# Layer A's output weights split ahead of time and kept in DRAM, and the bias rows of heads 4 to 15 written at another place

## The chip, the cores and the metric

The kernel runs on one core of one Trainium2 chip. The time is device microseconds (us) of one execution. Engines are called as in the profile: PE multiplies matrices (PEld is its weight load, which lies beside the matmuls), DVE, ACT and POOL work on vectors, SP here only issues DMAs. PE, DVE, ACT and POOL each work through their own instructions in order; so do the queues on which SP and POOL issue DMAs.

## The reference

A decoder of two layers over 1024 tokens of 1024 numbers, in float32. Layer A attends in three ways at once (over compressed blocks of keys, over chosen blocks, over a sliding window), adds the gated sum of the three through an output matrix, and runs a SwiGLU. Then one K/V is projected for layer B, whose heads attend over windows of three dilations. What the change touches is in these lines:

```python
def nsa_attention(h, w_in, ..., w_out, rel_bias):
    proj = h @ w_in                      # q, keys and values, gates
    ...
    k_cmp = compress(kvh(kc), pe_k, w1_k, w2_k)   # gelu(blocks @ w1) @ w2
    v_cmp = compress(kvh(vc), pe_v, w1_v, w2_v)
    ...                                  # every logit gets rel_bias[t5_bucket(distance)]
    o = g[..., 0:1] * o_cmp + g[..., 1:2] * o_sel + g[..., 2:3] * o_win
    return o.reshape(B, S, D_MODEL).astype(h.dtype) @ w_out
```

## The kernel before, in words

**Splits.** Every operand of a matmul is held as a high part (a rounded copy, made by ACT: `split` L139, `Pairs` L762) and a low part (operand minus high part, made by DVE: L140, L763; in a few places POOL). `mm3` (L166 to L168) makes one product of three matmuls: high by high, high by low, low by high.

**Order of the work.** The kernel is written as Python that records instructions. A scheduler then moves them within their dependencies by a model of the time. So the place of a call in the code isn't its place on an engine; where it stands there is shown below by rows of the order itself.

**Projections (0 to about 285 us).** `x` is normalised and turned, then multiplied by the column blocks of `a_w_in`. Weights come through the class `Weights`: SP loads 512 KB into a ring of three `wraw` tiles (L155), ACT and DVE split it into rings of five `wh` and `wl`. `tok_proj` makes values token by token (eight tiles of 128 tokens; 304 columns with the gates, then 256 columns); each tile is evacuated from one of six `mm` banks of PSUM by an ACT copy into `vt` (a ring of two), which POOL's queue stores to DRAM (`vS`). `compress` (L395 on) loads the compression weights in four quarters of 512 KB (`in_a_w_k_dram` in the rows below), makes for each of 16 chunks a split operand `bh`, `bl` (L410, L411) and adds six matmuls of 256 columns per chunk into the banks `cmp0` and `cmp1`; after them come the gelu (`hid`) and a second product.

**The bias rows.** `bias_rows` makes the bias by distance for all heads with four small matmuls (L252) and POOL's queue stores it to DRAM as `sR` (L254). `bias_skewed` (L256) then copies, for two heads at a time, one row of `sR` 128 times into the tensor `sA`, from which the attention reads slanted tiles (`T<-sA`). Each of the eight calls is one DMA of 1151 KB from DRAM to DRAM on SP's queue (L263). The argument `prev` ties it to a weight load: it can't be issued before that one.

**Attention A (about 285 to 745 us).** `jobs()` walks 32 units of four groups and eight tiles of tokens; a unit is `(g, t)`.

**Output product of A (about 745 to 845 us).** `out_proj` (L1048) loads `a_w_out` as eight tiles `ow`, and `rows_steps` (L789) multiplies the attention's output `oT` (left blocks) by `ow` (right blocks) in a recursion of seven products instead of eight. Each operand block of 128x512 goes through `Pairs` before use. Products three and four take sums of blocks: POOL makes them, four instructions on `oT` and four on `ow` (into `tb` or in place) for each product's preparation, L829 to L839. Results are added into `xr` by DVE (L821). The same function serves layer B later. The SwiGLU of layer A follows, and its first steps are placed among the recursion's last.

Of the kernel before, what the change touches and what calls it, by code (L numbers as in the profile page):

```python
# [10 lines left out]
F32 = mybir.dt.float32  # L11
F32R = mybir.dt.float32r
# [9 lines left out]
NT = S // 128  # L22
# [8 lines left out]
LA, L1, L2 = 1151, 511, 255  # L31
# [60 lines left out]
def trunk(ctx, tc, I, out):  # L92
    nc = tc.nc
# [249 lines left out]
    with ExitStack() as c:  # L343
# [95 lines left out]
        def evac_v(i):  # L439
# [6 lines left out]
            return f  # L446

        bias_rows(cp)
# [54 lines left out]
        for _ in steps:  # L503
            pass
        cctx.close()

# [11 lines left out]
    with ExitStack() as c:  # L518
# [190 lines left out]
        def jobs():  # L709
# [78 lines left out]

    def rows_steps(spare, pairs, tmp, blocks, xr):  # L789

# [3 lines left out]

        def step(ops, onX, where, sums=None, whole=False, eng=(None, None)):
# [29 lines left out]
        def sums1(i, a, b):  # L825
            (a11, a21, a12, a22), (b11, b12, b21, b22) = a, b
            tA.append(tmp("a", i))
            tB.append(tmp("b", i))
            nc.gpsimd.tensor_add(tA[i], a21, a22)  # L829
            nc.gpsimd.tensor_sub(tB[i], b12, b11)  # L830
            nc.gpsimd.tensor_sub(a21, a11, a21)
            nc.gpsimd.tensor_sub(b12, b22, b12)

        def sums2(i, a, b):
            (a11, a21, a12, a22), (b11, b12, b21, b22) = a, b
            nc.gpsimd.tensor_sub(tA[i], tA[i], a11)
            nc.gpsimd.tensor_sub(tB[i], b22, tB[i])
            nc.gpsimd.tensor_sub(a12, a12, tA[i])
            nc.gpsimd.tensor_sub(b21, b21, tB[i])  # L839

# [3 lines left out]
        T = lambda i: tA[i], lambda i: tB[i]  # L844
        return [step((A(0), B(0)), 1, [(0, 0)]),
                step((A(2), B(2)), 0, [(0, 0)]),
                step(T, 0, [(1, 1), (0, 1)], sums1),
                step(T, 2, [(0, 1)], sums2),
                step((A(2), B(3)), 0, [(0, 1)]),
                step((A(1), B(1)), 2, [(1, 1)], eng=(None, P)),  # L850
                step((A(3), B(2)), 2, [(1, 0)], whole=True, eng=(P, None))]

# [196 lines left out]
    def out_proj(pw, pp, p, xr, oT, w, x_src, norm):  # L1049
        raw = {k: pw.tile([128, 1024], F32, name=f"ow{k}") for k in (3, 7, 0, 4, 1, 5, 2, 6)}  # L1050
        for i in range(4):
            nc.sync.dma_start(raw[i], w[i * 128:(i + 1) * 128, :])
        for i in range(4):
            nc.sync.dma_start(xr[:, i, :], x_src[i * 128:(i + 1) * 128])
            nc.sync.dma_start(raw[i + 4], w[(i + 4) * 128:(i + 5) * 128, :])
        for t in range(4, NT):
            nc.sync.dma_start(xr[:, t, :], x_src[t * 128:(t + 1) * 128])
        lo, hi = slice(0, 512), slice(512, 1024)
        blocks = [((oT[:, i, lo], oT[:, i, hi], oT[:, i + 4, lo], oT[:, i + 4, hi]),
                   (raw[i][:, lo], raw[i][:, hi], raw[i + 4][:, lo], raw[i + 4][:, hi])) for i in range(4)]  # L1060
        steps = rows_steps(("dr0", "dr1", "ux", "uy"), Pairs(pp, 6),
                           lambda s, i: p.tile([128, 512], F32, name=f"t{s}{i}"), blocks, xr)
        staged(steps[:6] + [norm] + steps[6:])
# [301 lines left out]

    dense(0, I["a_w_out"][0], x_in, oT, (begin_B, project_B), "left", "right")
    oT_ctx.close()
# [297 lines left out]
```

## Time and profile before

| | us |
|---|---|
| time of three runs | 3013.38, 3022.8, 3020.68 (median 3020.68) |
| the profiled execution's own time | 3014.07 |
| its span in the profile | 3012.3 |
| PE busy | 2869.0 (95%) |
| DVE busy | 2405.6 (80%) |
| ACT busy | 1600.7 (53%) |
| POOL busy | 1640.1 (54%) |

The views used are: windows (busy time of each engine, with the count of instructions, in a stretch of time; behind them the mean granted clock of PE as a share of full speed, the busy share of the 16 DMA engines, and GB/s), groups (all instructions of one line, engine and shape: busy time, mean ns of one, and the idle time ahead of them with what ended it), tiles (count, then shortest/mean/longest ns, then first and last start), the timeline (start, length, engine, instruction; in brackets the idle time before it and what ended it), and DMA issues (count, KB of each, median us from issue to landing).

### The profile page before, as it was taken

Reading aid. Unit: us, or ns where it says so; the run is one execution under the profiler, and the core shown is the slowest. Engines: PE = TensorE matmul, PEld = TensorE weight load, DVE = VectorE, ACT = ScalarE, POOL = GpSimd, SP = SyncE. Lnnn points to the kernel's source line nnn. Section 1 sums busy time; section 2 is a strip of 40 time slices with the busy share of each in tenths; the row PEclk is TensorE's granted clock in tenths of the full one; section 3 lists DMA queues with packets and bytes.
Section 4 is the critical chain, followed back from the end, with each engine's and each line's share of the span. In section 5 each row is a group of like instructions: output and inputs, shape, how many; then the busy total and the mean of one; then the engine's idle time right before and its main releaser. Section 6 shows DMA issues by size and latency. Waiting matters only on the chain.

```text
span 3012.3 us, 44147 instructions
## 1 busy us (share of the span) xinstructions
PE 2869.0 (95%) x14670; PEld 2378.2 (79%) x14670; DVE 2405.6 (80%) x4832; ACT 1600.7 (53%) x3596; POOL 1640.1 (54%) x1751
## 2 busy tenths in 40 slices
PE   7999999999889999999999999899988999999997
PEld 6988888888667878888777788788866778888886
DVE  4432888988988898898875677588899788889887
ACT  5432888887363333333364444689964533333334
POOL 2134666666766555555556787333347655555551
PEclk9999999999999999999999999999999999999999
DMA  6765032121212223222124555866520212111111
GB/s 171 221 193 167 24 105 79 33 60 58 73 51 65 64 63 78 67 58 72 56 94 143 157 164 149 267 199 183 147 95 25 63 49 63 53 53 57 56 46 74
DMA packets 266196, 293.43 MB, mean 97 GB/s; under 512 B 17971, under 2 KB 209347, under 8 KB 265968
## 3 DMA queue, kind: packets, MB, share of 16 engines
q1 hardware_dynamic: 246320, 230.45, 26.6%
q0 software_dynamic: 19648, 60.16, 6.6%
q8 instruction: 116, 1.90, 0.3%
q14 instruction: 112, 0.92, 0.1%
HBM read 227.44 MB, written 78.81 MB: 102 GB/s over the span
## 4 chain that ended last, share of the span: by engine, by line
PE 61%; DVE 22%; ACT 6%; issue 5%; DMA 3%; POOL 2%; SPq 1%; DVEq 0%; ACTq 0%; POOLq 0%
DVE pl L763 7%; PE ux L166 5%; DVE xr L821 5%; PE ux L167 5%; PE ux L168 4%; PE pt L276 4%; PE uy L166 4%; PE uy L167 4%; PE uy L168 4%; PE dx L167 3%; PE mm L166 3%; PE dx L168 3%; PE mm L167 3%; PE mm L168 2%; PE dr L166 2%
## 5 line engine op out<-in xcount | busy, mean ns | idle before, releaser
L763 DVE TENSOR_TENSOR pl<-oT,ph 128x512 fp32r<-128x512 f32 x315 | 333.7, 1079 | 40.8 <-ACT ph L762 34.6
L762 ACT ACTIVATE ph<-oT 128x512 fp32r<-128x512 f32 x329 | 198.8, 626 | 222.3 <-PE ux L167 58.5
L276 PE MATMUL pt<-ident,P 128*128 128x128 f32 x1536 | 244.5, 278 | 10.9 <-ACT P L1459 2.7
L763 DVE TENSOR_TENSOR pl<-oTb,ph 128x512 fp32r<-128x512 f32 x229 | 228.1, 1021 | 24.0 <-ACT ph L762 23.9
L762 ACT ACTIVATE ph<-oTb 128x512 fp32r<-128x512 f32 x239 | 143.1, 625 | 185.4 <-PE ux L167 51.4
L821 DVE TENSOR_TENSOR xr<-xr,dr 128x512 f32<-128x512 f32 x336 | 214.4, 678 | 28.2 <-PE dr L168 28.1
L140 DVE TENSOR_TENSOR tl<-pt,th 128x512 fp32r<-128x512 f32 (+1 forms) x320 | 206.9, 651 | 30.8 <-ACT th L139 28.7
L821 DVE TENSOR_TENSOR xr<-xr,dx 128x512 f32<-128x512 f32 x352 | 220.1, 676 | 2.9 <-PE dx L168 2.2
L167 PE MATMUL dx<-pl,ph 128*128 128x512 f32 x512 | 203.2, 401 | 9.7 <-DVE pl L763 8.6
L689 POOL TENSOR_SCALAR P<-P,sm,gates 128x384 f32<-128x384 f32 (+7 forms) x256 | 182.5, 724 | 54.1 <-DVE sm L687 48.2
L276 PEld LDWEIGHTS pt<-ident,P 128*128 128x128 f32 x1536 | 179.6, 142 | 29.9 <-ACT P L1459 6.7
L168 PE MATMUL dx<-ph,pl 128*128 128x512 f32 x512 | 199.9, 397 | 0.3 <-DVE pl L763 0.3
L139 ACT ACTIVATE th<-pt 128x512 fp32r<-128x512 f32 (+1 forms) x320 | 176.8, 563 | 41.1 <-PE pt L276 35.2
L685 ACT ACTIVATE P<-P,m 128x384 f32<-128x384 f32 (+7 forms) x256 | 170.8, 669 | 16.2 <-DVE m L683 8.2
L1082 POOL TENSOR_TENSOR oT<-oT,gffn 128x512 f32<-128x512 f32 x92 | 108.2, 1183 | 128.7 <-DMA oT<-in_ffn_w_up_dram 112.4
L166 PE MATMUL dx<-ph 128*128 128x512 f32 x512 | 157.3, 398 | 8.4 <-DVE xr L821 3.3
L1082 POOL TENSOR_TENSOR oTb<-oTb,gffn 128x512 f32<-128x512 f32 x92 | 106.1, 1160 | 92.6 <-DMA oTb<-in_ffn_w_up_dram 83.1
L299 PE MATMUL o<-tl,V 128*128 128x256 f32 x540 | 147.6, 298 | 8.4 <-POOL tl L292 4.4
L298 PE MATMUL o<-th,V 128*128 128x256 f32 x540 | 149.6, 294 | 2.4 <-ACT th L139 1.3
L291 POOL TENSOR_SCALAR th<-traw 128x128 fp32r<-128x128 f32 (+1 forms) x112 | 74.8, 671 | 126.9 <-ACT traw L290 46.3
L1459 ACT ACTIVATE P<-P,st 128x384 f32<-128x384 f32 (+2 forms) x256 | 139.5, 547 | 7.7 <-PE pt L1570 4.1
L167 PEld LDWEIGHTS dx<-pl,ph 128*128 128x128 f32 x512 | 97.5, 190 | 40.7 <-DVE pl L763 21.1
(617 smaller groups left out, 9547.6 us busy)
## 6 DMA issues: line engine op xcount, KB each, us to landing
qB<-xr POOLq DMA_DIRECT2D x96, 256.0 KB, 4.9
oT<-in_ffn_w_up_dram SPq DMA_DIRECT2D x92, 256.0 KB, 3.0
oTb<-in_ffn_w_up_dram SPq DMA_DIRECT2D x92, 256.0 KB, 3.0
Q<-qB SPq DMA_DIRECT2D x40, 512.0 KB, 8.2
wd<-in_ffn_w_down_dram SPq DMA_DIRECT2D x66, 256.0 KB, 2.7
oT<-in_b_w_q_dram SPq DMA_DIRECT2D x48, 256.0 KB, 3.4
K<-kBs SPq DMA_DIRECT2D x40, 256.0 KB, 10.3
wraw<-in_a_w_in_dram SPq DMA_DIRECT2D x18, 512.0 KB, 5.0
```

Source lines behind the costliest of these rows:

```text
L139: nc.scalar.activation(H_, src, AF.Copy)
L140: nc.vector.tensor_sub(L_, src, f32(H_))
L166: nc.tensor.matmul(ps, lh, rh, start=first, stop=False, skip_group_check=bool(shared))
L167: nc.tensor.matmul(ps, lh, rl, start=False, stop=False, skip_group_check=bool(shared))
L168: return nc.tensor.matmul(ps, ll, rh, start=False, stop=last, skip_group_check=bool(shared))
L276: nc.tensor.transpose(ps[:, i * 128:(i + 1) * 128], b, ident)
L685: nc.scalar.activation(P[:, e, :n], P[:, e, :n], AF.Exp, bias=mm[:, e:e + 1], scale=-1.0, accum_out=sm[:, e:e + 1])
L689: nc.gpsimd.tensor_scalar(P[:, e, :n], P[:, e, :n], sm[:, e:e + 1], gt(g, t, br, 2 * hp + e, 1), op0=OP.mult, op1=OP.mult)
L762: nc.scalar.activation(h, src, AF.Copy)
L763: (eng or nc.vector).tensor_sub(l, src, f32(h))
L821: nc.vector.tensor_add(xs, xs, banks[t])
L1082: nc.gpsimd.tensor_mul(v, v, gains[:, k:k + 4].unsqueeze(2).to_broadcast([128, 4, 128]))
```

## The change

There are two parts.

First, a generator `prepared_out` runs in the projections. In four rounds it loads two tiles of `a_w_out` (`po0`, `po1`, 512 KB each, on SP), makes the four sums of the recursion with POOL, splits the seven blocks (28 in all, ACT and DVE, into a ring of three tiles `phl`), and stores each split block on POOL's queue into a new DRAM tensor `oP` (28 stores of 512 KB). `out_proj` of layer A then loads these 28 blocks (`oph`, a ring of eleven) on SP in place of eight `ow` tiles, and makes neither sums nor splits of the right operand. Layer B is as before.

Second, the calls of `bias_skewed` for heads 4 to 15 go from between the projections into the attention's `jobs()`, at the units (0,0), (0,3) and (1,3), two calls each, and with `prev` None, so that nothing but `sR` orders them.

```diff
+    oP = dram.tile([4, 7, 128, 2, 512], F32, name="oP")
+    def prepared_out(p):
+        lo, hi = slice(0, 512), slice(512, 1024)
+        for i in range(4):
+            top, low = [p.tile([128, 1024], F32, name=f"po{k}", bufs=1) for k in range(2)]
+            nc.sync.dma_start(top, I["a_w_out"][0][i * 128:(i + 1) * 128, :])
+            nc.sync.dma_start(low, I["a_w_out"][0][(i + 4) * 128:(i + 5) * 128, :])
+            b11, b12, b21, b22 = top[:, lo], top[:, hi], low[:, lo], low[:, hi]
+            def put(j, src):
+                t = p.tile([128, 2, 512], F32R, name="phl", bufs=3)
+                split(t[:, 0], t[:, 1], src)
+                nc.gpsimd.dma_start(oP[i, j], f32(t))
+            yield
+            for j, b in ((0, b11), (1, b21), (4, b22)):
+                put(j, b)
+            yield
+            t = p.tile([128, 512], F32, name="pot", bufs=1)
+            nc.gpsimd.tensor_sub(t, b12, b11)
+            put(2, t)
+            nc.gpsimd.tensor_sub(b12, b22, b12)
+            put(5, b12)
+            yield
+            nc.gpsimd.tensor_sub(b11, b22, t)
+            put(3, b11)
+            nc.gpsimd.tensor_sub(b21, b21, b11)
+            put(6, b21)
...
+        prep = prepared_out(pool(pctx, "pout", "right"))
         bias_rows(cp)
         tok_proj(wide(wts, W[:, 2304:2608], 304, 3), 304, hT, natural, evac_v(1))
+        next(prep)
...
         for _ in steps:
-            pass
+            next(prep)
...
             proj_T(blocks_weights(1, ch), hT, evac_c(kc2, ch))
-            bias_skewed(sA, 0, LA, WA + 1, 4 + 2 * ch, wts.last)
+            next(prep)
...
             f(*a)
-            bias_skewed(sA, 0, LA, WA + 1, 8 + 2 * n, wts.last)
+            next(prep, None)
...
                 g, t = u
+                for h in {(0, 0): (4, 6), (0, 3): (8, 10), (1, 3): (12, 14)}.get(u, ()):
+                    bias_skewed(sA, 0, LA, WA + 1, h, None)
...
-    def rows_steps(spare, pairs, tmp, blocks, xr):
+    def rows_steps(spare, pairs, tmp, blocks, xr, prepared=None):
...
             def operands(i):
+                right = prepared(i, j) if prepared else None
                 if sums is not None:
                     sums(i, *blocks[i])
-                return pairs(ops[0](i), eng[0]), pairs(ops[1](i), eng[1])
+                return pairs(ops[0](i), eng[0]), right or pairs(ops[1](i), eng[1])
...
+        if w is None:
+            ready = {}
+            def load(i, j):
+                t = ready[i, j] = pw.tile([128, 2, 512], F32R, name="oph", bufs=11)
+                nc.sync.dma_start(f32(t), oP[i, j])
...
-    dense(0, I["a_w_out"][0], x_in, oT, (begin_B, project_B), "left", "right")
+    dense(0, None, x_in, oT, (begin_B, project_B), "left", "right")
```

The scheduler moves more than the two parts say. On SP's queue in the projections, before, a copy of bias rows stood by itself between weight loads (in a row: line, operation, the tile with its number, the source, the shape; "x2" is two alike in a row):

```order
L155 DMA wraw_890<-in_a_w_in_dram 128x4x256
L155 DMA wraw_1129<-in_a_w_k_dram 128x4x256
L263 DMA sA<-sR 128x2x1151 x2
L155 DMA wraw_1175<-in_a_w_k_dram 128x4x256
L155 DMA wraw_1242<-in_a_w_in_dram 128x8x128
L263 DMA sA<-sR 128x2x1151
L155 DMA wraw_1307<-in_a_w_in_dram 128x8x128
```

On the same queue now, where `wraw_1206` is the fourth quarter of the key compression's weights, as `wraw_1175` was:

```order
L155 DMA wraw_910<-in_a_w_in_dram 128x4x256
L155 DMA wraw_1149<-in_a_w_k_dram 128x4x256
L340 DMA po_1448<-in_a_w_out_dram 128x1024
L341 DMA po_1449<-in_a_w_out_dram 128x1024
L263 DMA sA<-sR 128x2x1151 x8
L155 DMA wraw_1206<-in_a_w_k_dram 128x4x256
L155 DMA wraw_1299<-in_a_w_in_dram 128x8x128
```

All eight copies now stand in one piece in the projections, and the fourth quarter stands behind them; none is in the attention.

On PE, the fourth quarter was first used between products of the next column block (`wh_1243`, a block of the compressed values), before:

```order
L168 MATMUL mm<-hH_101,wl_1244 128x512
L166 MATMUL cmp_785<-bh,wh_1176 128x256
L166 MATMUL cmp_786<-bh,wh_1176 128x256
L167 MATMUL cmp_785<-bl,wh_1176 128x256
L168 MATMUL cmp_785<-bh,wl_1177 128x256
```

and it is now used ahead of that block, in the middle of the 256-column value projection (`wh_911` is its second half of weights):

```order
L166 MATMUL mm<-wh_911,hH_103 128x256
L167 MATMUL mm<-wl_912,hH_103 128x256
L168 MATMUL mm<-wh_911,hL_111 128x256
L166 MATMUL cmp_793<-bh,wh_1207 128x256
L167 MATMUL cmp_793<-bl,wh_1207 128x256
L166 MATMUL cmp_794<-bh,wh_1207 128x256
```

Counted in the order from the first 304-column matmul to that place, PE has 192 matmuls of the 304-column projection, 54 of the compression and 72 of the 256-column projection. Ahead of the first 304-column matmul PE had only the four small matmuls of the bias rows, before:

```order
L168 MATMUL mm<-hH_102,wl_278 128x512
L252 MATMUL mm<-oh,rb 16x512 x3
L252 MATMUL mm<-oh,rb 16x381
L166 MATMUL mm<-wh_523,hH_95 128x304
L167 MATMUL mm<-wl_524,hH_95 128x304
```

and now has 18 matmuls of the compression among them (the end of that piece):

```order
L166 MATMUL cmp_793<-bh,wh_796 128x256
L166 MATMUL cmp_794<-bh,wh_796 128x256
L252 MATMUL mm<-oh,rb 16x512
L167 MATMUL cmp_793<-bl,wh_796 128x256
L168 MATMUL cmp_793<-bh,wl_797 128x256
L167 MATMUL cmp_794<-bl,wh_796 128x256
L168 MATMUL cmp_794<-bh,wl_797 128x256
L252 MATMUL mm<-oh,rb 16x381
L166 MATMUL mm<-wh_527,hH_96 128x304
```

So 18 matmuls that wait for `bh` and `bl` now stand ahead of the 304-column projection.

More of the change, by code (lines that the diff above doesn't have):

```diff
@@ L464, in trunk @@
             proj_T(blocks_weights(1, ch), hT, evac_c(kc2, ch))
-            bias_skewed(sA, 0, LA, WA + 1, 4 + 2 * ch, wts.last)
+            next(prep)
         def evac_k(i, ch):
@@ L500, in trunk @@
             f(*a)
-            bias_skewed(sA, 0, LA, WA + 1, 8 + 2 * n, wts.last)
+            next(prep, None)
             next(steps, None)
         for _ in steps:
+            next(prep, None)
+        for _ in prep:
             pass
+        pctx.close()
         cctx.close()
@@ L787, in staged, with step @@
         run()
-    def rows_steps(spare, pairs, tmp, blocks, xr):
+    def rows_steps(spare, pairs, tmp, blocks, xr, prepared=None):
         X, tA, tB = [], [], []
         n = len(blocks)
-        def step(ops, onX, where, sums=None, whole=False, eng=(None, None)):
+        def step(j, ops, onX, where, sums=None, whole=False, eng=(None, None)):
             def operands(i):
+                right = prepared(i, j) if prepared else None
                 if sums is not None:
                     sums(i, *blocks[i])
-                return pairs(ops[0](i), eng[0]), pairs(ops[1](i), eng[1])
+                return pairs(ops[0](i), eng[0]), right or pairs(ops[1](i), eng[1])
             def prep():
@@ L825, in sums1 @@
         def sums1(i, a, b):
-            (a11, a21, a12, a22), (b11, b12, b21, b22) = a, b
+            a11, a21, a12, a22 = a
             tA.append(tmp("a", i))
-            tB.append(tmp("b", i))
             nc.gpsimd.tensor_add(tA[i], a21, a22)
-            nc.gpsimd.tensor_sub(tB[i], b12, b11)
+            if not prepared:
+                b11, b12, b21, b22 = b
+                tB.append(tmp("b", i))
+                nc.gpsimd.tensor_sub(tB[i], b12, b11)
+                nc.gpsimd.tensor_sub(b12, b22, b12)
             nc.gpsimd.tensor_sub(a21, a11, a21)
-            nc.gpsimd.tensor_sub(b12, b22, b12)
         def sums2(i, a, b):
-            (a11, a21, a12, a22), (b11, b12, b21, b22) = a, b
+            a11, a21, a12, a22 = a
             nc.gpsimd.tensor_sub(tA[i], tA[i], a11)
-            nc.gpsimd.tensor_sub(tB[i], b22, tB[i])
+            if not prepared:
+                b11, b12, b21, b22 = b
+                nc.gpsimd.tensor_sub(tB[i], b22, tB[i])
+                nc.gpsimd.tensor_sub(b21, b21, tB[i])
             nc.gpsimd.tensor_sub(a12, a12, tA[i])
-            nc.gpsimd.tensor_sub(b21, b21, tB[i])
         P = nc.gpsimd if n > 1 else None
@@ L844, in rows_steps @@
         T = lambda i: tA[i], lambda i: tB[i]
[L845 to L851, printed above, removed]
+        steps = [((A(0), B(0)), 1, [(0, 0)]),
+                 ((A(2), B(2)), 0, [(0, 0)]),
+                 (T, 0, [(1, 1), (0, 1)], sums1),
+                 (T, 2, [(0, 1)], sums2),
+                 ((A(2), B(3)), 0, [(0, 1)]),
+                 ((A(1), B(1)), 2, [(1, 1)], None, False, (None, P)),
+                 ((A(3), B(2)), 2, [(1, 0)], None, True, (P, None))]
+        return [step(j, *x) for j, x in enumerate(steps)]
     class Blocks:
@@ L1049, in out_proj @@
     def out_proj(pw, pp, p, xr, oT, w, x_src, norm):
[L1050 to L1057, printed above, removed]
@@ L1058, in out_proj, with load_x @@
-        lo, hi = slice(0, 512), slice(512, 1024)
-        blocks = [((oT[:, i, lo], oT[:, i, hi], oT[:, i + 4, lo], oT[:, i + 4, hi]),
-                   (raw[i][:, lo], raw[i][:, hi], raw[i + 4][:, lo], raw[i + 4][:, hi])) for i in range(4)]
+        lo, hi = slice(0, 512), slice(512, 1024)
+        left = [(oT[:, i, lo], oT[:, i, hi], oT[:, i + 4, lo], oT[:, i + 4, hi]) for i in range(4)]
+        def load_x(ts):
+            for t in ts:
+                nc.sync.dma_start(xr[:, t, :], x_src[t * 128:(t + 1) * 128])
@@ new lines, in out_proj, with prepared @@
+        if w is None:
[3 more added lines that the diff above has]
+                nc.sync.dma_start(f32(t), oP[i, j])
+            for n in range(8):
+                load(n % 4, n // 4)
+                if n == 3:
+                    load_x(range(4))
+            load_x(range(4, NT))
+            def prepared(i, j):
+                if (i, j) not in ready:
+                    load(i, j)
+                t = ready[i, j]
+                return t[:, 0], t[:, 1]
+            blocks = [(a, None) for a in left]
+        else:
+            prepared = None
+            raw = {k: pw.tile([128, 1024], F32, name=f"ow{k}") for k in (3, 7, 0, 4, 1, 5, 2, 6)}
+            for i in range(4):
+                nc.sync.dma_start(raw[i], w[i * 128:(i + 1) * 128, :])
+            for i in range(4):
+                load_x((i,))
+                nc.sync.dma_start(raw[i + 4], w[(i + 4) * 128:(i + 5) * 128, :])
+            load_x(range(4, NT))
+            blocks = [(left[i], (raw[i][:, lo], raw[i][:, hi], raw[i + 4][:, lo], raw[i + 4][:, hi]))
+                      for i in range(4)]
@@ L1061, in out_proj @@
         steps = rows_steps(("dr0", "dr1", "ux", "uy"), Pairs(pp, 6),
-                           lambda s, i: p.tile([128, 512], F32, name=f"t{s}{i}"), blocks, xr)
+                           lambda s, i: p.tile([128, 512], F32, name=f"t{s}{i}"), blocks, xr, prepared)
         staged(steps[:6] + [norm] + steps[6:])
```

1 line of the change is left out of this document (added).

## Prediction

> **What bounds the kernel now.** I read the page first, then windows over the stages of layer A, then the timeline, tiles and DMA issues at the places that the change touches.
>
> ```profile
> span 3012.3 us, 44147 instructions
> PE 2869.0 (95%) x14670; PEld 2378.2 (79%) x14670; DVE 2405.6 (80%) x4832; ACT 1600.7 (53%) x3596; POOL 1640.1 (54%) x1751
> ```
>
> PE is busy 95% of the span, so time can only be won where PE waits or runs at a low clock, and any new wait of PE is paid in full. The windows say where that is: start-up, the rest of the projections, attention A, output product A, start of its SwiGLU (columns: stretch, length, busy and count of PE, PEld, DVE, ACT, POOL, PE clock, DMA share, GB/s).
>
> ```profile
> 0.00:60.00 60.00, 43.39 (x201) 34.46 (x202) 35.15 (x64) 36.74 (x72) 16.91 (x28) 0.92 0.59 166
> 60.00:285.00 225.00, 225.00 (x1257) 197.96 (x1256) 76.17 (x113) 72.67 (x111) 60.61 (x124) 1.00 0.68 196
> 285.00:745.00 460.00, 446.49 (x2933) 384.38 (x2931) 392.69 (x1595) 385.93 (x1128) 300.66 (x491) 0.98 0.21 60
> 745.00:845.00 100.00, 87.75 (x368) 68.49 (x368) 91.90 (x108) 45.19 (x87) 72.75 (x49) 0.95 0.22 80
> 845.00:905.00 60.00, 51.21 (x247) 39.67 (x246) 50.32 (x71) 39.14 (x75) 40.98 (x32) 0.97 0.21 62
> ```
>
> The projections from 60 to 285 us have no idle PE at all: nothing can be won there, everything can be lost. DVE, ACT and POOL are a third busy there, so the added splits and sums have room. In the output product PE is idle for 12.25 us of 100, DVE is busy for 91.9, and the clock is 0.95. That is the stage that the prepared weights relieve. So the change takes work from a stage that waits and puts it, with 14.7 MB of stores, into a stage that doesn't; and it gathers the bias copies in front of a weight load.
>
> **Term 1: start of the token projection.** The first 304-column matmul stood at 57.63, with nothing of the compression ahead of it; now 18 compression matmuls stand ahead.
>
> ```profile
> 57.63 0.62 PE L166 MATMUL mm<-wh,hH 128*128 128x304 f32 x1
> 59.32 1.39 ACT L410 ACTIVATE bh<-kc,pet 128x256 fp32r<-128x256 f32 x2 [1.31 <-DVE kc L357]
> L410 ACT ACTIVATE bh<-kc,pet x20: 731/742/756, 59.3 to 155.8; 128x256 fp32r<-128x256 f32 x20
> L411 DVE SCALAR_TENSOR_TENSOR bl<-kc,pet,bh x20: 652/664/689, 60.1 to 157.1; 128x256 fp32r<-128x256 f32 x20
> ```
>
> They need three pairs of `bh` and `bl`, and the first `bh` begins at 59.32, when DVE has filled `kc`. Three copies of 0.74 and the last subtraction of 0.66 end at 62.2; with a split of the output weights between them on ACT, and two more `po` loads ahead of `x` in the start-up, I put the projection at 65, 7 us later. The 18 matmuls are then done, 2.1 us of work (18 by 0.118, below). Cost 5, from 0 (everything ready earlier in the new order) to 9.
>
> **Term 2: the fourth quarter behind eight copies.** Let S be the start of the token projection. PE reaches the fourth quarter after 192, 54 and 72 matmuls.
>
> ```profile
> 86.07 0.28 PE L166 MATMUL cmp<-bh,wh 128*128 128x256 f32 x1
> 88.00:115.00 27.00, 27.00 (x228) 27.00 (x227) 11.18 (x19) 11.01 (x17) 3.25 (x6) 1.00 0.97 285
> ```
>
> Before, the 192 took from 57.63 to 86.07, 28.4 us; 228 matmuls of 256 columns took 27.00, 0.118 each, so 126 take 14.9. PE needs the quarter at S+43. When is it there? The copies start when `sR` lands:
>
> ```profile
> 58.85 0.51 POOL L254 DMA_DIRECT2D sR<-R  x1 [3.77 <-DVE R L253]
> 61.65 1.29 SPq L263 DMA_DIRECT2D sA<-sR  x2
> sA<-sR SPq DMA_DIRECT2D x1, 1151.0 KB, 8.3
> sA<-sR SPq DMA_DIRECT2D x2, 1151.0 KB, 11.5
> 61.00:77.00 16.00, 16.00 (x117) 16.00 (x116) 2.02 (x7) 1.22 (x4) 1.68 (x3) 1.00 0.73 181
> ```
>
> The first two copies were issued together at 61.65, 4 us after the projection's start (the two DMA rows: the first alone, then both). The first landed after 8.3; with a median of 11.5 the second landed after 14.7, 6.4 later. Eight in a row then take 8.3 + 7 x 6.4 = 53, and the last lands at S+57. A load queued behind a copy landed soon after it:
>
> ```profile
> 119.43 0.58 SPq L263 DMA_DIRECT2D sA<-sR  x1
> 120.15 0.52 SPq L155 DMA_DIRECT2D wraw<-in_a_w_v_dram  x1
> sA<-sR SPq DMA_DIRECT2D x1, 1151.0 KB, 10.1
> wraw<-in_a_w_v_dram SPq DMA_DIRECT2D x1, 512.0 KB, 11.2
> L139 ACT ACTIVATE wh<-wraw x19: 696/1057/1089, 9.0 to 153.7; 128x1024 fp32r<-128x1024 f32 x16, 128x912 fp32r<-128x912 f32 x2, 128x608 fp32r<-128x608 f32 x1
> L140 DVE TENSOR_TENSOR wl<-wraw,wh x19: 793/1225/1227, 10.1 to 154.8; 128x1024 fp32r<-128x1024 f32 x16, 128x912 fp32r<-128x912 f32 x2, 128x608 fp32r<-128x608 f32 x1
> ```
>
> Copy at 119.43 + 10.1 = 129.5, load at 120.15 + 11.2 = 131.4: 1.8 behind. With the split, 1.06 and 1.23, the quarter is ready at S+61. PE stops for 18 us. Eight stores of `phl` lie in the same time (counted in the order between `sR` and that use), and they aren't in the measured pair. Two rows bound them:
>
> ```profile
> xS<-xr POOLq DMA_DIRECT2D x8, 512.0 KB, 3.0
> 210.00:240.00 30.00, 30.00 (x140) 24.87 (x139) 7.87 (x10) 5.85 (x10) 14.75 (x34) 1.00 1.06 337
> ```
>
> A store of that size lands in 3.0 by itself, so it may slip in between; at the 285 GB/s of the full stretch above, eight of 0.52 MB take 15 more. I take 20 for the stop, near the measured pair, with an upper end of 35. The lower end: if the eight copies went at the best rate of the projections, 337 GB/s, their 9.43 MB would take 28 us, the quarter would be ready at S+38, and PE wouldn't stop. Point of decision: a burst of 37 us or less costs nothing.
>
> The Trainium skill, "DMA: Bandwidth & Descriptors", section "Queues, rings and completion order", says that a DMA engine takes turns between the queues that have work, a packet at a time. By that rule the stores don't wait behind the copies but take their share, and this term would be at its upper end, 35; the 285 GB/s with all engines busy is the row that bears on it, and it can't decide between 20 and 35.
>
> **Term 3: restart.** After a stop the clock has to come back. In the output product, behind a wait, it was granted at 0.66 for 10 us:
>
> ```profile
> 765.00:775.00 10.00, 5.92 (x15) 3.90 (x13) 9.97 (x10) 1.74 (x4) 10.00 (x8) 0.66 0.09 26
> 769.25 0.79 PE L167 MATMUL dr<-pl,ph 128*128 128x512 f32 x1 [3.72 <-DVE pl L763]
> 795.00:800.00 5.00, 2.37 (x7) 1.91 (x8) 5.00 (x7) 0.00 (x0) 5.00 (x5) 0.83 0.20 56
> ```
>
> A third of 10 us is 3; the gelu behind the quarter now queues after two more splits on ACT, 2 more. I take 5, from 0 to 8.
>
> **Term 4: attention.** Its order on PE is the same, and no copy lies in it. Nothing, both ways; `sA` is written before it begins either way.
>
> **Term 5: the output product.** DVE loses the 28 low parts less four, ACT 28 copies, POOL four low parts and 16 sums.
>
> ```profile
> L762 ACT ACTIVATE ph<-ow x40: 612/616/629, 747.4 to 2320.8; 128x512 fp32r<-128x512 f32 x40
> L763 DVE TENSOR_TENSOR pl<-ow,ph 128x512 fp32r<-128x512 f32 x16 | 21.7, 1356 | 2.6 <-ACT ph L762 2.6
> L763 DVE TENSOR_TENSOR pl<-tb,ph 128x512 fp32r<-128x512 f32 x8 | 11.7, 1467 | 0.0
> L763 DVE TENSOR_TENSOR pl<-oT,ph 128x512 fp32r<-128x512 f32 x16 | 19.6, 1231 | 2.7 <-ACT ph L762 2.6
> L830 POOL TENSOR_TENSOR tb<-ow 128x512 f32<-128x512 f32 x4 | 6.9, 1741 | 0.0
> 748.04 1.19 PE L166 MATMUL dx<-ph 128*128 128x512 f32 x4 [2.04 <-ACT ph L762]
> 797.63 0.50 PE L167 MATMUL dx<-pl,ph 128*128 128x512 f32 x1 [2.77 <-DVE pl L763]
> ```
>
> 21.7 + 11.7 = 33.4 us of DVE's 91.9 go, and with 16 sums of about 1.7 some 27 us of POOL. DVE then has 58 us of work in the stage and no longer bounds it; PE does. PE's 12.25 of idle time and the clock's 5% of 87.75, 4.4, are 16.6 together; what stays is the wait for the left operand's first split (2.04 here) and a few like it. I take -14. Bounds: -5 if PE goes on waiting for the left operands, whose low parts still cost 1.2 us each, or for the 28 loads; -22 if most of the 8.8 us that PE idles from 845 to 905 goes as well.
>
> **Sum.** 5 + 20 + 5 + 0 - 14 = +16, made against the profiled execution's own 3014.07: 3030.1. The median of the runs is 6.6 above it, 3020.68; on that footing the forecast is 3036.7, **3037**. This kernel's measurement can tell about 0.3%, 9.1 us: faster means under 3011.6, slower over 3029.7.
>
> **The rivals.** *The burst is short (chance 0.15).* For it: 337 GB/s from 210 to 240 us, with all kinds of DMA under way. Against it: the pair of copies with the 181 GB/s of its stretch. Then PE doesn't stop: 5 + 0 + 2 - 14 = -7, 3014, within 0.3% or a little faster. It decides at the 37 us above. The Trainium skill, the page just named, section on the anatomy of one DMA, fits a DMA's time by 2.0 us plus its bytes at 436 GB/s; an estimate by that is 4.7 us for a copy and 24 for eight, which is this rival. The trace disagrees: 8.3 for the first, 6.4 for the next.
>
> *ACT is held by stores (0.12).* A ring of three `phl` and one of two `vt` both wait for stores that share the DMA engines with the copies. It was seen once under two copies:
>
> ```profile
> 75.23 0.38 ACT L139 ACTIVATE vt<-mm 128x256 fp32r<-128x256 f32 x1 [8.70 <-DMA vS<-vt]
> ```
>
> Six `mm` banks by 3.55 us a tile (28.4 / 8) cover 21 us, so that one cost nothing. Three such waits in a row would use the cover up, and PE would stop for one more of them, about 9 us: 3045.
>
> *Short burst and a quicker start of the SwiGLU (0.07).* No stop, and term 5 at its upper end: 5 + 0 + 2 - 22 = -15, 3006, faster.
>
> That the change doesn't do what it says holds for its second part: by the order nothing of the copying lies in the attention. That is in the forecast, not beside it.
>
> **How the numbers follow.** The forecast has 0.63: its own range, from the terms' ends, is 3024 to 3054. The rivals have 0.15, 0.12 and 0.07; 0.03 is left for what I don't see. For 8 in 10 the range reaches from the short burst (3012) to the upper end of term 2 with a late restart (3058). Faster: the third rival and a third of the first, 0.12. Same: the rest of the first and the forecast's low end, 0.18. Slower: 0.70.
>
> **What would show it.** In the changed kernel's profile: `sA` as one group of eight, the last landing some 53 us after the first issue; a wait of PE of about 20 us on `wh` or `wraw` at a `cmp` matmul some 43 us into the token projection, with a low clock behind it; attention as long as before, 460 us; the output product with DVE well under 90 of 100 and PE without the waits of 2 to 4 us on `pl`. I am wrong if PE doesn't stop there (then the copies went faster than the pair says), or if the output product gains nothing, which would mean that the left operands or the loads bounded it.

## The result, and the profile after

The changed kernel took 3047.28 us (median of 4 runs, 3042.92 to 3056.67), the kernel before 3017.03 (4 runs, 3012.62 to 3022.8). The ratio is 1.0103, 95% interval 1.0072 to 1.0135: about 31 us slower. The profiled execution took 3042.92, its span is 3041.2.

The page of the changed kernel, first lines:

```profile
span 3041.2 us, 44323 instructions
PE 2874.8 (95%) x14670; PEld 2381.3 (78%) x14670; DVE 2394.6 (79%) x4836; ACT 1604.0 (53%) x3597; POOL 1646.1 (54%) x1775
```

PE's work is the same as before to 6 us, and the span is 29 longer: the time is in waits and in a lower clock. The windows of the changed kernel, cut where its stages now begin (columns as in the prediction):

```profile
0.00:60.00 60.00, 39.19 (x188) 31.33 (x188) 41.78 (x65) 40.16 (x77) 31.55 (x43) 0.89 0.82 260
60.00:333.00 273.00, 242.32 (x1265) 208.35 (x1266) 101.25 (x141) 86.60 (x133) 83.47 (x151) 0.92 0.70 209
333.00:791.00 458.00, 443.94 (x2936) 381.86 (x2935) 394.07 (x1595) 386.23 (x1128) 303.39 (x494) 0.99 0.21 56
791.00:868.00 77.00, 76.01 (x340) 62.72 (x341) 50.05 (x80) 27.24 (x51) 34.28 (x26) 0.98 0.71 266
868.00:933.00 65.00, 56.87 (x274) 44.25 (x273) 51.40 (x72) 42.71 (x82) 44.62 (x33) 0.97 0.20 57
```

The projections, which had no idle PE, now have 31 us of it in the second row, at a clock of 0.92. The output product has lost its waits: PE busy 76.01 of 77, DVE 50.05 where it had been the bound.

A more exact reading takes the same matmul in both traces and subtracts its starts. Two such anchors, the first and last score of the attention's compressed branch, before and then after (tile rows; the last two numbers are the first and last start):

```profile
L601 PE MATMUL s<-kc,Q x256: 217/275/421, 286.6 to 694.2; 128*128 128x64 f32 x128
```

```profile
L639 PE MATMUL s<-kc,Q x256: 217/275/323, 335.1 to 739.7; 128*128 128x64 f32 x128
```

The attention begins 48.5 us late and at its last score is 45.5 late: all the loss lies ahead of it, in the start-up and the projections. The same subtraction at six places, for all kernels of this study (worked out from the traces, us against the profile of before; the last column is the span):

```
                token    attention  output   SwiGLU's  layer B's  last     span
                proj.    begins     product  5th prod. attention  matmul
before, start    57.6     286.6     748.0     889.9     1910.2    2995.8   3012.3
changed kernel  +17.4     +48.5     +44.5     +27.7      +35.0     +33.3    +28.9
bias_only        +2.3     +17.2     +18.7     +18.7      +14.5     +16.2    +16.2
bias_back       +16.5     +32.2     +34.7     +16.3      +20.9     +18.3    +13.9
bias_late       +16.3     +16.3     +42.2     +23.8      +28.7     +30.6    +26.2
late_held        +2.0     +10.3     +11.6      -6.7       +2.5      +3.1     -1.3
after_held       +3.1     +30.5     +34.0     +15.6      +22.0     +19.0    +14.6
back_held        +0.1      +8.5     +33.2     +14.9      +22.3     +24.6    +20.2
held_addr        +0.1     +10.1     +10.4      -8.1       -4.2      -2.8     -7.2
back_held2       -0.3      +9.3      +6.4     -12.0      -10.5      -8.6    -13.0
after_dve        +7.3     +35.2     +35.7     +18.5      +25.6     +29.0    +24.6
held2_dve        +0.4      +2.7      +3.7     -13.1       -7.8      -6.7    -11.0
held2_sums       +0.3      +9.0     +12.7      -5.8       +0.3      -1.5     -5.9
held2_both       +0.8      +1.3      +1.6     -16.9      -14.1     -12.9    -17.3
```

Each line is one execution of one kernel. Among the kernels whose attention has PE's order of before, the attention runs from 4.0 us shorter than before (the changed kernel) to 3.7 longer (held2_sums), so a difference of a few us between two lines shows nothing by itself.

**The stop.** The changed kernel around the fourth quarter: SP's queue, the PE row where it stops, ACT's row ahead of it, and the two DMA rows.

```profile
75.06 0.62 PE L166 MATMUL mm<-wh,hH 128*128 128x304 f32 x1
81.45 20.19 SPq L263 DMA_DIRECT2D sA<-sR  x8
104.56 0.38 SPq L155 DMA_DIRECT2D wraw<-in_a_w_k_dram  x1
138.00 1.06 ACT L139 ACTIVATE wh<-wraw 128x1024 fp32r<-128x1024 f32 x1 [19.96 <-DMA wraw<-in_a_w_k_dram]
139.11 0.58 PE L166 MATMUL cmp<-bh,wh 128*128 128x256 f32 x1 [16.63 <-ACT wh L139]
sA<-sR SPq DMA_DIRECT2D x8, 1151.0 KB, 33.1
wraw<-in_a_w_k_dram SPq DMA_DIRECT2D x1, 512.0 KB, 33.4
```

The copies go out from 81.45, S+6.4 (S, as in the prediction, is the start of the token projection, 75.06 here); the quarter behind them lands at 104.56 + 33.4 = 138.0, S+62.9, and PE goes on at S+64, after 16.63 us. The clock then takes its time:

```profile
130.00:135.00 5.00, 0.00 (x0) 0.00 (x0) 0.00 (x0) 0.00 (x0) 0.00 (x0) 0.50 1.03 301
140.00:145.00 5.00, 4.96 (x24) 4.54 (x24) 4.39 (x7) 3.90 (x7) 1.70 (x2) 0.53 1.03 335
145.00:155.00 10.00, 7.06 (x45) 6.48 (x44) 7.22 (x12) 6.65 (x12) 6.77 (x10) 0.83 0.57 218
```

In 130 to 135 no engine works and the DMA engines are full. PE then works at half clock until 145, and from 145 to 155 it idles 2.9 of 10 us, part of it for the gelu's results.

**The late start.** The token projection begins at 75.06, not at 65. What came late is `kc` and so `bh`: the changed kernel's DVE, POOL, ACT and PE ahead of it.

```profile
55.82 3.82 DVE L140 TENSOR_TENSOR wl<-wraw,wh 128x1024 fp32r<-128x1024 f32 x1 [1.78 <-ACT wh L139]
56.03 1.30 POOL L356 TENSOR_TENSOR po<-po,po 128x512 f32<-128x512 f32 x1
57.28 1.27 POOL L359 TENSOR_TENSOR po<-po,pot 128x512 f32<-128x512 f32 x1
65.83 1.39 ACT L441 ACTIVATE bh<-kc,pet 128x256 fp32r<-128x256 f32 x2 [1.77 <-DVE kc L388]
66.62 0.80 PE L166 MATMUL cmp<-bh,wh 128*128 128x256 f32 x2 [7.63 <-ACT bh L441]
70.00:80.00 10.00, 10.00 (x32) 6.61 (x32) 5.08 (x8) 3.13 (x5) 3.44 (x5) 0.51 0.65 193
```

A weight split that took DVE 1.23 us before took 3.82. POOL's two sums of the output weights lie inside it, from 56.03 to 58.55; the 0.21 ahead of them and the 1.09 behind them are about its own time, and 1.23 and the two sums' 2.57 are 3.80. The first `bh` began 6.5 later than before (65.83 against 59.32). PE waited 7.63 for it and then ran ten microseconds at a clock of 0.51.

**The output product.** Where the trace of before named DVE's low parts as what PE waits for (before, then after; waits of PE in 745 to 845 and in 791 to 868: total, times, longest):

```profile
PE dx L167 <- DVE pl L763: 4.6, 6, 2.8
PE dr L167 <- DVE pl L763: 4.5, 3, 3.7
PE dx L166 <- ACT ph L762: 2.7, 2, 2.0
```

```profile
PE dx L166 <- ACT ph L802: 1.0, 1, 1.0
L803 DVE TENSOR_TENSOR pl<-oT,ph 128x512 fp32r<-128x512 f32 x16 | 12.5, 810 | 10.2 <-ACT ph L802 7.0 <-PE dx L167 3.1
```

One wait is left, the first operand's, and a low part of `oT` takes 810 ns where it took 1231.

### The profile page after: what moved, and what is told of

It is laid out like the page before. It is cut to its first block, busy times and chain, and to the rows that moved or that the text cites. A ratio compares the mean times of both kernels' runs of the same rounds, so it can differ in the third digit from the quotient of the medians.

```text
span 3041.2 us, 44323 instructions
## 1 busy us (share of the span) xinstructions
PE 2874.8 (95%) x14670; PEld 2381.3 (78%) x14670; DVE 2394.6 (79%) x4836; ACT 1604.0 (53%) x3597; POOL 1646.1 (54%) x1775
## 4 chain that ended last, share of the span: by engine, by line
PE 64%; DVE 19%; ACT 5%; issue 5%; DMA 4%; POOL 2%; SPq 1%; DVEq 0%; ACTq 0%; POOLq 0%
PE ux L166 5%; DVE pl L803 5%; PE ux L167 5%; PE ux L168 5%; PE pt L276 4%; DVE xr L862 4%; PE uy L166 4%; PE uy L167 4%; PE uy L168 4%; PE dx L167 3%; PE dx L168 3%; PE dx L166 3%; PE dr L166 2%; PE mm L166 2%; PE mm L167 2%
## 5 line engine op out<-in xcount | busy, mean ns | idle before, releaser
L803 DVE TENSOR_TENSOR pl<-oT,ph 128x512 fp32r<-128x512 f32 x315 | 324.4, 1050 | 45.9 <-ACT ph L802 36.9
L167 PE MATMUL dx<-pl,ph 128*128 128x512 f32 x448 | 178.9, 401 | 5.4 <-DVE pl L803 4.2
L168 PE MATMUL dx<-ph,pl 128*128 128x512 f32 x448 | 175.6, 396 | 0.0
L166 PE MATMUL dx<-ph 128*128 128x512 f32 x448 | 138.4, 399 | 5.8 <-DVE xr L862 5.2
L1527 DVE CUSTOM_DVE_ANT_0 P<-s,T 128x384 f32<-128x384 f32 (+2 forms) x256 | 114.2, 473 | 11.4 <-PE pt L276 7.2
```

Of the source, the lines that this page charges most:

```text
L166: nc.tensor.matmul(ps, lh, rh, start=first, stop=False, skip_group_check=bool(shared))
L167: nc.tensor.matmul(ps, lh, rl, start=False, stop=False, skip_group_check=bool(shared))
L168: return nc.tensor.matmul(ps, ll, rh, start=False, stop=last, skip_group_check=bool(shared))
L803: (eng or nc.vector).tensor_sub(l, src, f32(h))
```

## The experiments

My theory after the result: two separate losses in the projections, the late start (prepared work in the start-up) and the stop (the copies in one piece), against a gain in the output product. Rivals: that the preparing itself costs PE time all through, that copies or stores alone make the stop, that copies in the attention would hold it up. All ratios are to the kernel before, timed in the same session, with 95% intervals.

**bias_only**: before, with the second part alone.

```diff
-            bias_skewed(sA, 0, LA, WA + 1, 4 + 2 * ch, wts.last)
-            bias_skewed(sA, 0, LA, WA + 1, 8 + 2 * n, wts.last)
+                for h in {(0, 0): (4, 6), (0, 3): (8, 10), (1, 3): (12, 14)}.get(u, ()):
+                    bias_skewed(sA, 0, LA, WA + 1, h, None)
```

> The kernel before with the change's second part alone: heads 4 to 15 copied in one piece of eight, no prepared weights. My theory: the copies take 53 to 57 us from their issue, as in the changed kernel, but here the order needs what lies behind them later (first the next block's weights, some 59 us into the token projection, by 192 matmuls of 304 columns, 72 + 192 of 256), and the copies start 4 us into it, so PE stops for about 6 us: 6 to 8 us slower than before, start and output product unchanged. Rival 1, the copies by themselves cost the whole stop whatever the order: 25 to 30 us slower. Rival 2, the copies are only long because the stores of split weights run beside them: no stop, no difference.

1.0053 (1.0037 to 1.0068), 16 us slower: between theory and rival 1, and rival 2 falls, since PE stops without any stores of split weights. The profile, at the stop:

```profile
63.62 14.87 SPq L263 DMA_DIRECT2D sA<-sR  x8
111.66 1.06 ACT L139 ACTIVATE wh<-wraw 128x1024 fp32r<-128x1024 f32 x1 [14.51 <-DMA wraw<-in_a_w_k_dram]
112.62 0.73 ACT L410 ACTIVATE bh<-kc,pet 128x256 fp32r<-128x256 f32 x1
PE cmp L166 <- ACT bh L410: 10.1, 1, 10.1
```

I had counted when PE needs the quarter. But ACT works in order: the quarter's split stood ahead of a `bh` that PE needed earlier, and PE waited for that `bh`, 10.1 us. With the low clock behind it the projections are 15 us longer. From the first copy's issue to the quarter's landing it is 48 us here, against 56.5 in the changed kernel.

**bias_back**: the changed kernel, copies back between the projections.

```diff
+            bias_skewed(sA, 0, LA, WA + 1, 4 + 2 * ch, wts.last)
+            bias_skewed(sA, 0, LA, WA + 1, 8 + 2 * n, wts.last)
...
-                for h in {(0, 0): (4, 6), (0, 3): (8, 10), (1, 3): (12, 14)}.get(u, ()):
-                    bias_skewed(sA, 0, LA, WA + 1, h, None)
```

> The changed kernel with the copies of heads 4 to 15 put back between the projections, the prepared weights kept. My theory: the start of the token projection stays about 15 us late (the splits and loads of output weights in the start-up), no stop at the fourth quarter, the output product and the SwiGLU's start gain 18 us as in the changed kernel: 0 to 5 us faster than before. Rival 1, splits and stores cost PE time all through the projections whatever the copies do: 15 to 30 us slower than before. Rival 2, the late start is itself caused by the copies: the start is as before, 15 to 20 us faster.

1.0063 (1.0044 to 1.0082), slower than I expected. The start is late by 16.5, so rival 2 falls; the projections then lose 16 more with no stop at the quarter: in the table, +16.5 becomes +32.2. PE's longest wait there is 5.0 us, for the gelu's result. The whole is 19 us slower, which is rival 1's number, though the next run shows that the preparing alone doesn't cost it.

**bias_late**: the changed kernel, copies tied into the attention.

```diff
-            nc.sync.dma_start(f32(t_), ...)                  # a load of V
+            grp["last"] = nc.sync.dma_start(f32(t_), ...)
...
-                    bias_skewed(sA, 0, LA, WA + 1, h, None)
+                    bias_skewed(sA, 0, LA, WA + 1, h, grp["last"])   # the last V load issued
```

> The changed kernel with the copies of heads 4 to 15 tied behind a load of the attention, two at a time, so that they lie in the attention as the code has them. My theory: start 15 us late, no stop in the projections, output product 18 us better, attention 0 to 5 us longer: within 5 us of before. Rival 1, as above, the prepared work costs PE time all through: 15 to 30 us slower. Rival 2, six copies on the queue ahead of the attention's loads hold PE up: attention 10 to 25 us longer.

1.0086 (1.0063 to 1.0109). The projections are as the theory says: late by 16.3 at their start and 16.3 at their end, no stop. Two of the six copies still go out in them, at 236; four lie in the attention. But the attention is 26 us longer, which looks like rival 2. That it isn't shows at back_held.

**late_held**: as bias_late, and the loads of output weights tied behind weight loads.

```diff
+            with after(wts.last):
                 nc.sync.dma_start(top, ...)
                 nc.sync.dma_start(low, ...)
-        next(prep)          # the first two calls, in the token projection
-        next(prep)
```

> As the one with late copies, and the loads of output weights are tied behind weight loads, the first behind that of the third quarter, so that nothing of the preparing lies in the start-up. My theory: the start is as before, no stop, output product and SwiGLU's start 18 us better: 13 to 18 us faster than before. Rival 1, the late start comes back as waits in the projections, since the same splits and stores then lie between weight splits: 0 to 5 us faster at most. Rival 2, the gain of the output product hangs on the clock or on chance and not on the prepared weights: no difference.

0.9987 (0.9974 to 1.0000). The start is as before (+2.0), the output product gains 18 (+11.6 to -6.7), the projections lose 8 after their start: rival 1's number, and so no clear gain. The attention, with the same copies in it as bias_late, is 1.3 us longer than before.

**after_held**: the changed kernel, eight copies in one piece, loads held as in late_held.

> The changed kernel, the eight copies still in one piece, with the loads of output weights tied behind weight loads so that the start-up is as before. My theory, two separate losses in the changed kernel, the late start (15 us) and the stop behind the copies: start 2 us late at most, a stop of 10 to 17 us some 43 us into the token projection with 5 to 6 us of low clock behind it, output product 18 to 19 us better, K/V stage 7 to 11 us worse as in each run with prepared weights: 8 to 13 us slower than before. Rival, one loss (the late start only gave the copies less to hide): the stop grows by what the start gains, 25 to 30 us slower.

1.0046 (1.0027 to 1.0066): 14 us slower. The late start goes (+3.1), the stop stays, and they are two losses, not one:

```profile
64.49 18.28 SPq L263 DMA_DIRECT2D sA<-sR  x8
121.15 0.58 PE L166 MATMUL cmp<-bh,wh 128*128 128x256 f32 x1 [11.73 <-ACT wh L139]
```

**back_held**: bias_back, loads held.

> Copies between the projections as before, prepared weights kept, their loads tied behind weight loads. My theory: as the run with late copies and held loads, projections about 10 us longer by splits that stand ahead of bh on ACT and wait for their loads, output product 18 to 19 us better, K/V 7 to 11 worse: 0 to 5 us faster than before. Rival, copies and stores of split blocks together fill the DMA engines: projections 18 to 25 us longer, 3 to 10 us slower.

1.0054 (1.0037 to 1.0072), 16 us slower, which neither the theory nor the rival had. Projections +8.5 as in the theory; but the attention is 25 us longer, with no copy in it. That bears on bias_late. The attention's 2928 matmuls can be set beside those of before, place by place, by tiles and shapes. In late_held, the changed kernel, bias_back and all the others but four, all 2928 agree. In bias_late and back_held only 1488 and 1486 do, while these two agree with each other in 2926. So the scheduler laid the attention out in another way in these two, the same way in both, and with this layout it is 25 us longer, whether copies lie in it or not. Late_held, with the same copies and the layout of before, is 1.3 longer. (bias_only and after_dve share a third layout, with 2627 places as before, which cost 1.5 and 0.5.) The longest waits of bias_late's PE there are on other engines' softmax and splits, and none is on a DMA:

```profile
PE pt L276 <- DVE tl L140: 5.9, 7, 2.4
PE o L298 <- POOL th L291: 5.1, 5, 3.0
PE pt L679 <- DVE mk L677: 4.8, 4, 1.7
```

What tips the scheduler was not looked into.

**held_addr**: late_held, with layer B's DRAM tensors declared ahead of `oP`.

```diff
+    xS = ...; qB = ...; kBs = ...; vBs = ...    # moved up from layer B
     oP = dram.tile([4, 7, 128, 2, 512], F32, name="oP")
```

> The run with late copies and held loads, with the DRAM tensors of layer B (xS, qB, kBs, vBs) declared ahead of oP, so that they lie where they lay before the change; no instruction moves. Theory A, the 7 to 11 us that the K/V stage lost in each run with prepared weights come from the place of these tensors in DRAM: they go, 10 to 13 us faster than before. Theory B, they come from the different phase of DVE and POOL work there: within 3 us of the run it is made from, 3 us faster than before.

0.9976 (0.9960 to 0.9992), within reach of both. In the table, from the SwiGLU to layer B's attention, it goes from -8.1 to -4.2, late_held from -6.7 to +2.5. A loss of 4 is left, so theory A in its full form isn't borne out; and as the runs without this edit lose anything from 1.5 to 9 there, in one execution each, the 4 shows no part of it either.

**back_held2**: back_held, and the preparing begins only behind the key compression.

```diff
         for _ in steps:
-            next(prep)
+            pass
```

> Copies as before, and the preparing begins only with the column blocks behind the key compression, its loads tied behind weight loads. My theory: no split stands in the token projection, so the projections are 0 to 4 us longer, output product 18 to 19 us better, K/V 7 to 11 worse: 6 to 12 us faster than before. Rival, splits ahead of bh hold PE up at the value compression instead: projections 10 us longer, no difference from before.

0.9978 (0.9966 to 0.9991), 7 us faster: the lower end of the theory. The start is before's (-0.3). The loss in the projections (+9.3) is as large as the rival says, but lies in two main places. Each matmul's start-to-start, beside the usual one of its shape before, gives 3.7 us too much from 98 to 112, at the end of the key compression, and 4.3 from 175 to 200, in the value compression; PE's waits there are for `bl`, which DVE makes.

**after_dve**: the changed kernel, the preparing's sixteen sums on DVE in place of POOL.

```diff
-            nc.gpsimd.tensor_sub(t, b12, b11)
+            nc.vector.tensor_sub(t, b12, b11)      # and the three others
```

> The changed kernel with the sixteen sums of the preparing made by DVE in place of POOL. In the changed kernel DVE operations that run beside these sums on POOL took up to three times as long (a weight split 3.82 us). Theory A, that slowing is most of the late start: the token projection starts 6 to 9 us late in place of 17, the whole is 20 to 24 us slower than before. Theory B, the loads ahead of x and the splits that stand in the queues are most of it: the start stays 13 to 17 us late, 26 to 31 us slower. The stop behind the eight copies stays in both.

1.0052 (1.0033 to 1.0071), 16 us slower, less than either theory has. The start is 7.3 late in place of 17.4, the number of theory A, and the weight split takes its usual time. But the first `bh` is as late as in the changed kernel:

```profile
57.00 1.22 DVE L140 TENSOR_TENSOR wl<-wraw,wh 128x1024 fp32r<-128x1024 f32 x1 [3.73 <-ACT wh L139]
64.93 0.62 PE L166 MATMUL mm<-wh,hH 128*128 128x304 f32 x1
65.51 1.39 ACT L441 ACTIVATE bh<-kc,pet 128x256 fp32r<-128x256 f32 x2 [2.18 <-DVE kc L388]
```

So theory A isn't shown for the start. The scheduler put the 18 compression matmuls behind the projection's beginning again, and the projection no longer waits for `bh`; `bh` itself, 6.2 late in place of 6.5, gained nothing from sums on DVE. For the projections behind the start the next run is the cleaner test.

**held2_dve**: back_held2 with that same edit.

> The run with copies as before and late, held preparing, its sixteen sums made by DVE in place of POOL. Theory A, as above: the projections are 4 to 6 us longer than before in place of 9, 10 to 13 us faster than before. Theory B, what is lost there is the splits' place in the queues: within 2 us of the run it is made from, about 7 us faster than before.

0.9945 (0.9924 to 0.9966), 16 us faster (10 to 23 by the interval): theory A's gain or more. The start is before's in both, and the loss in the projections falls from 9.3 to 2.7: POOL's sums, slowing DVE, were most of what the preparing cost PE. The edit also moved 112 of the 1462 matmuls ahead of the attention, so part of the 6.6 can be the order's. In back_held2 the longest low part of `phl` took 3237 ns, here 694 (tile rows, the first back_held2's; the middle number of a tile row is the median, not the mean):

```profile
L140 DVE TENSOR_TENSOR phl<-po,phl x24: 668/682/3237, 99.9 to 226.6; 128x512 fp32r<-128x512 f32 x24
```

```profile
L140 DVE TENSOR_TENSOR phl<-po,phl x24: 673/684/694, 101.4 to 211.7; 128x512 fp32r<-128x512 f32 x24
```

**held2_sums**: back_held2, with POOL's sums of layer B and of the down product in their former order.

```diff
                 nc.gpsimd.tensor_sub(tB[i], b12, b11)
-                nc.gpsimd.tensor_sub(b12, b22, b12)
             nc.gpsimd.tensor_sub(a21, a11, a21)
+            if not prepared:
+                nc.gpsimd.tensor_sub(b12, b22, b12)
...                                           # and alike in the next round of sums
```

> The run with copies as before and late, held preparing, with the sums of the down product and of layer B's output product on POOL in the order that they had before the change. If that order is why the K/V stage loses 5 to 11 us in each run with prepared weights: 12 to 16 us faster than before. If it is only the phase of DVE and POOL work, which any edit shifts: within 3 us of the run it is made from, 4 to 10 us faster than before.

0.9978 (0.9964 to 0.9992): the same as back_held2. Layer B wasn't quite as before in the changed kernel: POOL made these sums in another order there. The order of these sums isn't the cause of the K/V stage's loss.

**held2_both**: both edits.

> Both edits of the two runs before, DVE for the sums of the preparing and the former order of the other sums. If each works: 14 to 19 us faster than before; if neither does: 4 to 10 us faster.

0.9950 (0.9934 to 0.9966), 2999.73 us beside 3014.5: the first edit's gain, not more. It beats both kernels of this case. Its windows over projections and output product:

```profile
60.00:288.00 228.00, 227.86 (x1266) 200.18 (x1264) 102.82 (x158) 87.85 (x139) 76.89 (x154) 0.99 0.86 277
750.00:831.00 81.00, 81.00 (x373) 66.96 (x372) 54.81 (x86) 32.69 (x65) 38.17 (x29) 1.00 0.65 246
```

The 28 splits, 16 sums and 14.7 MB of stores lie in the projections beside a PE that all but never waits (0.14 us), and the output product runs without a wait at full clock.

## Why the prediction was right, and where it wasn't

The direction, the mechanism and the range held: 3047.28 lies between 3012 and 3058, and PE stops where and for what the prediction said. The middle was 10 us low, and by the table 13 on the profiled execution (+28.9 against +16). That it wasn't further off is partly luck. By the table, some 29 us of loss weren't in the sum (10 in term 1, 12 in term 3, 7 between the SwiGLU and layer B's attention), and some 16 that went the other way weren't either (3 in the stop, 4 in the attention, 3 in term 5, 6 from there to the end). Term by term:

*Term 1, the start, forecast 5, measured 17.4 less the 2.1 of matmuls done ahead: 15.3.* This is one of two steps that failed. The forecast took the first `bh` from the row of before, 59.32; it began at 65.83, and the 18 matmuls behind it ran at a clock of 0.51. I priced the added splits and sums by their own durations and said DVE, ACT and POOL have room. The start-up isn't the stretch that has room (DVE 35 of 60 us before), and a sum on POOL isn't free for DVE beside it: the split of 3.82 us waited out two of them. The Trainium skill says this in "SBUF — State Buffer", section "SBUF: two separate sides": DVE and POOL share a pair of ports that is a lock for a whole instruction and not a shared rate. The 3.80 above agrees, and I hadn't drawn on it. The rows don't show which of the two has the ports first: DVE's begins 0.21 ahead of the first sum, and it is DVE that waits. The held runs show that the whole delay belongs to preparing in the start-up (start +0 to +3; in them the 18 matmuls don't stand ahead either). How the 6.5 of `bh` divide between the loads, splits and sums there stays open, since with the sums on DVE it was 6.2 late as well. That POOL's sums cost PE time in the projections proper is what held2_dve shows.

*Term 2, the stop, forecast 20 (18 from the pair of copies), measured 16.63.* Right in its mechanism and near in its steps: first copy S+4 against S+6.4, copies and quarter 53 + 1.8 against 56.5, PE's need S+43 against S+47, ready S+61 against S+64. But the 53 holds by errors that cancel. The pair's second copy landed 7.0 us behind the first, not 6.4, since it was issued 0.65 later; with that the sum is 57. The copies by themselves are quicker than the pair: in bias_only eight took 46.6, and 48.0 with the quarter. The stores, which the 18 leaves out, make it 55.1 and 56.5. (The lower end's S+38 is also S+36 by its own figures, 4 + 28 + 1.8 + 1.06 + 1.23.) The stores' share can be read from bias_only: 48 without those of split weights, 56 with; POOL's queue moved 5.2 MB in that stretch against 1.3, SP's 10.8 against 10.5. The Trainium skill's rule from "DMA: Bandwidth & Descriptors", section "Queues, rings and completion order", that an engine takes turns between queues, agrees in kind, since the stores do lengthen what is queued on SP; but by 8 us here, not the 15 that would have made the term 35. The first rival, no stop, is out: eight copies took 46.6 by themselves. The fit of the Trainium skill's same page, in "Anatomy of one DMA — SWDGE (gpsimd) path", gives an estimate of 24 us for them; the page measured it on DMAs that POOL issues, and these are SP's.

*Term 3, the restart, forecast 5; what the projections lose beside terms 1 and 2 is 16.6* (48.5 less 15.3 and 16.63). This is the other step that failed. The two parts that had a price came out: the half clock from 139 to 145 cost 2.9, the gelu's results 1.5. The sum had nothing for other waits and further spells of low clock. Each matmul's start-to-start, beside the usual one of its shape before, gives 2.2 us too much from 75 to 80 at a clock of 0.52 (before, 1.3 at that place), 3.2 from 105 to 120 in the blocks of compression matmuls, which wait for `bl` at every second chunk, 5.0 from 145 to 155 (the gelu's 1.5 among them, a wait for `gates`, and a clock of 0.66 from 150), and 3.8 from 155 to 170, most of it one wait for `vt`. PE's waits beside the two long ones:

```profile
PE mm L166 <- DVE vt L140: 2.8, 1, 2.8
PE mm L166 <- DVE gates L476: 1.9, 2, 1.4
PE cmp L166 <- ACT hh L139: 1.2, 1, 1.2
PE cmp L167 <- DVE bl L442: 0.6, 3, 0.2
```

*Term 4, attention, forecast 0, measured -4* (48.5 at its beginning, 44.5 at its end), no more than single executions differ by.

*Term 5, the output product, forecast -14, measured -16.8* (44.5 to 27.7), and 16.8 to 18.5 in every run with prepared weights; 0 in bias_only. The 28 loads didn't hold it back at 266 GB/s.

*What wasn't forecast:* from the SwiGLU to layer B's attention the changed kernel loses 7.3 us, with PE's order the same. Each run with prepared weights loses between 1.5 and 9 there, bias_only gains 4. Neither the tensors' place in DRAM nor the order of POOL's sums explains it by itself; the cause stays open. And from the last matmul to the end it is 12.1 us in place of 16.5, in every run with prepared weights and not in bias_only, which wasn't looked into.

The rival of ACT held by stores didn't happen in its own form: from 60 to 175 ACT's `vt` copies waited 12.5 us for stores, against 24.0 before. In a small way it may have: shortly before the `vt` for which PE waited 2.8 us, ACT had stood 3.9 and 0.9 us for stores. Its idea, head of line on ACT, did decide bias_only: a split that waits for its load held up the `bh` behind it.

## What to carry to other kernels

Before work is moved into a stage "with room", look at the stretch where it will lie, not at the stage's mean, and ask which engine shares its time: between back_held2 and held2_dve, sixteen sums on POOL went with 6.6 us of PE's loss, and the 28 splits and 28 stores, with the sums on DVE, with 2.7. A call's place in scheduled code isn't its place on the chip: copies without a tie went into the queue as soon as `sR` was there, ahead of a load that PE needed. And when an edit changes a stage that it doesn't touch, compare the order of that stage before explaining the time: the 25 us of the attention came with another layout by the scheduler.

## What the runs showed of the hardware that I had not expected

A DVE subtraction of two tiles in SBUF beside POOL's sums isn't slowed by a share, it waits them out. Another case, in back_held2, DVE and POOL:

```profile
175.10 3.24 DVE L140 TENSOR_TENSOR phl<-po,phl 128x512 fp32r<-128x512 f32 x1 [1.32 <-DMA kS<-stl]
175.22 1.31 POOL L357 TENSOR_TENSOR po<-po,po 128x512 f32<-128x512 f32 x1
176.48 1.29 POOL L360 TENSOR_TENSOR po<-po,pot 128x512 f32<-128x512 f32 x1
```

0.68 for the low part by itself (the median above) and the two sums, 175.22 to 177.77, make 3.23. A subtraction that reads one operand from a bank of PSUM (`mm`) didn't wait in the same kernel, with 0.47 us of a sum beside it:

```profile
211.37 1.31 POOL L362 TENSOR_TENSOR po<-po,po 128x512 f32<-128x512 f32 x1
212.21 0.69 DVE L140 TENSOR_TENSOR stl<-mm,sth 128x512 fp32r<-128x512 f32 x1 [1.13 <-ACT sth L139]
```

In the output product before, where DVE has one low part after another, POOL's sums are longer too, 1.74 us where the shortest took 1.28.

Eight DRAM-to-DRAM copies of 1151 KB and the load behind them took 48 us in one queue, and 56 with stores of 512 KB beside them. And after 16.6 us without a matmul the granted clock was 0.50 and stayed at about half for some 6 us of work (0.53 from 139 to 145).
